# A gMLP and dilated-attention trunk: all operand differences on VectorE, inputs loaded in order of use, and the value norm's root on GpSimd

## The chip, the cores and the metric

The kernel runs on one core of a Trainium2 chip. A core has five engines that work side by side, each in the order of its own queue: TensorE (PE, matmuls), VectorE (DVE), ScalarE (ACT), GpSimd (POOL) and SyncE (SP, which issues DMAs here). They wait for each other through semaphores. The metric is the device time of one execution in microseconds (us). A figure before and a figure after are medians of several executions.

## The reference, cut to what matters

Two layers over 1024 positions with 1024 channels, all in fp32. Layer 0 mixes positions with a gated MLP, layer 1 with dilated attention; each is followed by a dense MLP, and a norm ends it.

```python
for layer in range(DEPTH):                       # DEPTH = 2
    y = _rms_norm(h, mix_norm_g[layer])
    if layer % 2 == 0:
        uv = gelu(y @ w_in); u, v = split(uv)    # the "value" half is v
        v = _layer_norm(v, ln_g, ln_b)
        mixed = einsum('gts,bnsgc->bntgc', tril(w_s), v) + b_s
        y = (u * mixed) @ w_out
    else:
        y = _dilated_attention_mixer(y, ...)     # q, k, v = y @ w_qkv; three dilations; merge; @ w_out
    h = h + y
    y = _rms_norm(h, mlp_norm_g[layer])
    h = h + square(relu(y @ w_up[layer])) @ w_down[layer]
return _rms_norm(h, final_norm_g)
```

`_rms_norm` divides by the root of the mean square plus 1e-6.

## The kernel before, in words

**Numbers.** Each fp32 operand is split into a high part (ACT copies it to the matmul's format) and a low part (DVE subtracts). A product takes three matmuls: high×high, high×low, low×high. A `weight` or `pair().split(...)` therefore costs an ACT and a DVE instruction on a tile of 128x512. `whi`/`wlo` and `wp` are split weights, `y` and `t` split activations, `r` are raw weights as loaded (a pool of four buffers), `h` is the residual, `keep` and `raws` normalized activations, `t…` temporaries of a pool of 11.

**Banks.** Results go to PSUM banks of two pools: `mm` (3) and `at` (5). A bank is free again when ACT or DVE has taken its result out.

**Start.** x arrives transposed, in halves (512 positions) of 8 blocks `h0`…`h7`. The value half v is made in three passes (`gi` 0, 1, 2) over groups of output tiles; the first two also read x. In each of the eight steps k of a pass, `scaled(s, k)` multiplies a block of x with the norm's weights into `y` (and its square into a sum: `Square`, the sums on POOL), two weight halves are loaded and split, and 18 matmuls of 512 columns follow. The norm's 1/rms is not put into y. It is made at the end of the pass (`rms`, four small matmuls, then `rsqrt`) and goes as the scale `rs` into the Gelus (`v_out`), which free the banks for the next pass. `gate_weights` loads and splits the matrices w_s (`wsh`/`wsl`) and makes the bias rows `rb`; `spatial` uses them.

**Seven products.** From the first MLP on, large products are made as seven half-size products in place of eight, with sums and differences of blocks of the operands. `Terms` forms those of the activations: `first` for the first half of the positions (kept in `keep`), `second` for the second half (in `raws`), then four differences for each of four tiles, then `rest`, the splits left over. There are three such stages: before the first MLP, before the attention, before the second MLP. Before the seven products begin, four tiles of each half are made the `classical` way, and their results are evicted (in the MLP `squared`: Relu, Square). Weight sums for the seven products are formed on POOL (`Weights`, L401 to L406). `first_sum` (L750) copies the first product's result out of its bank, for which the next product waits. In the attention, `out` evicts q, k and V tiles (L1079, L1122), a `Unit` is one block of heads: scores from q and k, softmax (L1217, L1219), transposes with `ident`, values.

**Order.** PE's order is written by hand: `Flow` runs generators beside the main loop and places their matmuls by fixed latencies (`LAT`). For the other engines a scheduler picks from what is ready, by priorities; `tc.high_priority(offset=PRIO)` puts an instruction forward. Each engine then works strictly in the order found.

## Time and profile before

| what | value |
| --- | --- |
| median of 3 executions | 2182.33 us (2180.11 to 2182.43) |
| the profiled execution: its time, its span | 2182.13 us, 2180.4 us |
| PE busy | 2121.8 us, 97% of the span |
| DVE, ACT, POOL busy | 1647.1, 1126.3, 600.9 us |
| bytes moved by DMA | 247.04 MB, mean 113 GB/s |
| mean TensorE clock granted | 0.99 |

The profile is one execution. Its span is the stretch from the first to the last instruction. A row of the timeline reads: start, length, engine, line, operation, tile written <- tiles read, shape, number of instructions, and in brackets how long the engine stood idle before and what ended that. `PEclk` in a table by windows is the share of full clock that PE was granted.

### The profile page before, as it was taken

How to read it: one execution, taken by the hardware profiler on the slowest of the kernel's cores; microseconds unless marked ns; L12 is line 12 of the kernel's file. 1: busy time of each engine (PE TensorE's matmuls, PEld its weight loads, DVE VectorE, ACT ScalarE, POOL GpSimd, SP SyncE). 2: the span in 40 equal slices, each digit the busy share in tenths (PEclk: the TensorE clock that was granted, in tenths of full speed). 3: DMA queues.
4: the chain of work that ended last, by engine and by line, in shares of the span. 5: the costliest groups of instructions: out<-in, count | busy, mean ns of one | idle time of the engine just before them, and what ended most of it. 6: DMA issues, size and time to landing. Idle time of an engine off the chain costs nothing.

```text
span 2180.4 us, 30158 instructions
## 1 busy us (share of the span) xinstructions
PE 2121.8 (97%) x10242; PEld 1755.2 (80%) x10242; DVE 1647.1 (76%) x2987; ACT 1126.3 (52%) x2266; POOL 600.9 (28%) x442
## 2 busy tenths in 40 slices
PE   7999999999999999998999999999999999999998
PEld 5888887888878888886888788887878888788887
DVE  5875349676689888878787877878786666988886
ACT  5743225555564444346665656665455555544443
POOL 1100115333223322533212222201343232333345
PEclk9999999999999999999999999999999999999999
DMA  6221213456354444321211111141055543644432
GB/s 222 87 88 45 62 41 96 158 189 198 138 176 160 159 141 137 105 82 39 52 46 46 43 48 45 46 147 62 20 169 193 184 159 113 203 150 146 157 104 78
DMA packets 158814, 247.04 MB, mean 113 GB/s; under 512 B 33481, under 2 KB 47940, under 8 KB 158660
## 3 DMA queue, kind: packets, MB, share of 16 engines
q1 hardware_dynamic: 157760, 243.89, 34.3%
q8 instruction: 80, 1.31, 0.2%
q10 hardware_dynamic: 900, 1.23, 0.2%
q14 instruction: 74, 0.61, 0.1%
HBM read 180.41 MB, written 64.66 MB: 112 GB/s over the span
## 4 chain that ended last, share of the span: by engine, by line
PE 82%; DVE 9%; ACT 3%; issue 2%; DMA 2%; POOL 0%; SPq 0%; DVEq 0%; ACTq 0%; POOLq 0%
PE at L180 41%; PE mm L180 39%; PE at L187 2%; DVE wp L204 2%; DVE t L204 1%; ACT t L1219 1%; ACT wp L203 1%; DVE k L1122 1%; DMA t<-hid 1%; DVE tr L204 0%; DMA r<-in_w_v 0%; DVE h L332 0%; DVE q L1122 0%; DVE h L893 0%; DMA h<-hd 0%
## 5 line engine op out<-in xcount | busy, mean ns | idle before, releaser
L203 ACT ACTIVATE wp<-r 128x512 fp32r<-128x512 f32 (+3 forms) x492 | 295.1, 605 | 458.0 <-PE at L180 287.7
L180 PE MATMUL mm<-y,wp 128*128 128x512 f32 x1608 | 405.2, 398 | 12.8 <-ACT t L750 6.6
L180 PE MATMUL at<-hx,wp 128*128 128x512 f32 x1770 | 413.8, 390 | 3.8 <-DVE wp L204 2.2
L204 DVE TENSOR_TENSOR wp<-r,wp 128x512 fp32r<-128x512 f32 (+3 forms) x492 | 380.9, 778 | 40.1 <-ACT wp L203 36.3
L180 PEld LDWEIGHTS at<-hx,wp 128*128 128x128 f32 x1770 | 331.8, 188 | 75.1 <-DVE h L893 3.3
L180 PEld LDWEIGHTS mm<-y,wp 128*128 128x128 f32 x1608 | 303.2, 191 | 80.4 <-ACT t L750 7.5
L180 PE MATMUL at<-t,wp 128*128 128x512 f32 x1344 | 314.3, 389 | 0.0
L180 PEld LDWEIGHTS at<-t,wp 128*128 128x128 f32 x1344 | 252.7, 188 | 52.7 <-DVE t L756 0.2
L401 POOL TENSOR_TENSOR t<-r 128x512 f32<-128x512 f32 (+3 forms) x78 | 112.8, 1446 | 624.8 <-DMA r<-in_w_dn 270.3
L403 POOL TENSOR_TENSOR r<-r 128x512 f32<-128x512 f32 (+3 forms) x78 | 118.4, 1518 | 326.9 <-DVE wp L204 320.1
L180 PE MATMUL mm<-t,wp 128*128 128x512 f32 x768 | 192.6, 398 | 0.0
L204 DVE TENSOR_TENSOR hx<-t,hx 128x512 fp32r<-128x512 f32 x192 | 179.8, 948 | 5.7 <-ACT hx L203 5.6
L261 POOL TENSOR_TENSOR t<-t 128x512 f32<-128x512 f32 (+1 forms) x54 | 69.1, 1280 | 387.3 <-ACT t L252 385.4
L180 PE MATMUL mm<-hx,wp 128*128 128x512 f32 x708 | 171.8, 389 | 0.0
L180 PEld LDWEIGHTS mm<-t,wp 128*128 128x128 f32 x768 | 141.2, 189 | 29.8
L180 PE MATMUL mm<-y,whi 128*128 128x512 f32 x512 | 158.1, 390 | 0.0
L180 PEld LDWEIGHTS mm<-hx,wp 128*128 128x128 f32 x708 | 132.8, 188 | 28.1 <-DVE b L919 0.6
L893 DVE TENSOR_TENSOR h<-h,at 128x512 f32<-128x512 f32 x144 | 97.5, 679 | 55.4 <-PE at L180 55.3
L180 PE MATMUL at<-y,wp 128*128 128x512 f32 x552 | 138.1, 391 | 0.0
L756 DVE TENSOR_TENSOR t<-t,at 128x512 f32<-128x512 f32 x116 | 79.0, 683 | 74.9 <-PE at L180 74.7
L203 ACT ACTIVATE hx<-t 128x512 fp32r<-128x512 f32 x192 | 118.4, 628 | 27.8 <-DMA t<-hid 23.4
L406 POOL TENSOR_TENSOR r<-r 128x512 f32<-128x512 f32 (+3 forms) x78 | 107.2, 1374 | 79.8 <-issue 54.0
(213 smaller groups left out, 3244.0 us busy)
## 6 DMA issues: line engine op xcount, KB each, us to landing
t<-hid SPq DMA_DIRECT2D x194, 256.0 KB, 5.0
hid<-t SPq DMA_DIRECT2D x140, 256.0 KB, 2.7
r<-in_w_up SPq DMA_DIRECT2D x128, 256.0 KB, 2.8
r<-in_w_dn SPq DMA_DIRECT2D x88, 256.0 KB, 2.7
r<-in_w_qkv SPq DMA_DIRECT2D x72, 256.0 KB, 2.6
hid<-b SPq DMA_DIRECT2D x56, 256.0 KB, 2.7
r<-in_w_v SPq DMA_DIRECT2D x48, 256.0 KB, 3.0
h<-in_xT SPq DMA_DIRECT2D x16, 256.0 KB, 4.5
```

The costliest lines, as they stand in the source:

```text
L180: nc.tensor.matmul(out, lhsT, rhs, **kw)
L187: nc.tensor.transpose(out, src, ident)
L203: nc.scalar.activation(hi, src, AF.Copy)
L204: nc.vector.tensor_tensor(lo, src, hi.bitcast(F32), op=ALU.subtract)
L261: nc.gpsimd.tensor_tensor(self.acc, self.acc, sq, op=ALU.add)
L401: tt(r3, r[0, 0], r[1, 0], op=ALU.subtract)
L403: tt(r[1, 1], r[1, 0], r[0, 0], op=ALU.subtract)
L406: tt(r[0, 0], r[0, 1], r[1, 1], op=ALU.subtract)
L756: nc.vector.tensor_tensor(out, x, y, op=ALU.add)
L893: engine.tensor_tensor(hs[i, s], hs[i, s], src, op=ALU.add)
L1122: nc.vector.scalar_tensor_tensor(lo, a, sc, hi.bitcast(F32), op0=ALU.mult, op1=ALU.subtract)
L1219: nc.scalar.activation(p[:, c], p[:, c], AF.Exp, bias=m, scale=-1.0, accum_out=dn)
```

## The change

1. `rsqrt(..., power=True)` for the first two value norms: in place of Sqrt on ACT and reciprocal on DVE, POOL raises the mean square to the power −0.5 (one instruction on 128x4); the two refinement steps on DVE stay. The norm is made after the first tile of the last step, not after the second.
2. DMAs at the start: block of x, weight half, weight half for each step; the second half of x later; gate weights and their biases by SP after the first pass (before: by ACT's queue within it), and their splits and bias rows within the second pass, put forward. `spatial` waits for `rb_done`.
3. In the second pass the weights of steps 2 to 7 are split behind the sixth Gelu; `scaled` is one step ahead.
4. `Terms.second`: all sixteen differences on DVE, terms 6 and 7 first; `rest` waits for them and splits terms 5 and 4. The copy on POOL goes. Temporaries take the place of spare tiles.
5. MLP: the four Relus first, put forward, then the Squares.
6. The spill of h to memory stands elsewhere in the program; its DMAs have the same neighbours in SP's queue as before.
7. Attention: the second half's tiles are evicted in the order 2, 3, 0, 1.

Where rows differ, the first place is the end of the first pass, on ACT. `whi_556` and, in the new names, `whi_505` are the weights of the second pass's step k=1, `sd` is the root, `vg` the Gelus' output, `rs` the scale. Before:

```order
L203 ACTIVATE whi_556<-r_557 128x512 [waits DMAHW2_49,DVE_49,PE_49]
L203 ACTIVATE whi_556<-r_561 128x512 [waits DMAHW3_49]
L231 ACT_TABLE_LOAD
L231 ACTIVATE sd_417<-at_412,scalars_89 128x4 [waits PE_49]
L588 ACT_TABLE_LOAD
L588 ACTIVATE vg_433<-at_121,rs_104 128x512 [waits DVE_49]
L588 ACTIVATE vg_433<-at_122,rs_104 128x512
```

Now:

```order
L205 ACTIVATE whi_505<-r_510 128x512 [waits DMAHW4_49]
L618 ACT_TABLE_LOAD [waits DVE_49]
L618 ACTIVATE vg_414<-at_123,rs_106 128x512 [waits PE_49]
L618 ACTIVATE vg_414<-at_124,rs_106 128x512 [waits PE_49]
L618 ACTIVATE vg_417<-at_125,rs_106 128x512 [waits PE_49]
L618 ACTIVATE vg_417<-mm_126,rs_106 128x512 [waits PE_49]
```

The root and one table load are gone. The wait for the scale (a DVE semaphore) stood on the first Gelu and stands now on the table load ahead of it.

The start of SP's queue; `h0` to `h2` are blocks of x, `r` weight halves. Before:

```order
L508 DMA h0_92<-in_xT 128x512
L169 DMA r_113<-in_w_v 128x512
L169 DMA r_117<-in_w_v 128x512
L169 DMA r_154<-in_w_v 128x512
L508 DMA h1_93<-in_xT 128x512
L169 DMA r_158<-in_w_v 128x512
L169 DMA r_196<-in_w_v 128x512 [waits DMAHW2_49,DMAHW0_49,DVE_49]
L169 DMA r_200<-in_w_v 128x512 [waits DMAHW3_49,DMAHW1_49,DVE_49]
L169 DMA r_244<-in_w_v 128x512 [waits DMAHW5_49,DVE_49]
```

Now:

```order
L521 DMA h0_94<-in_xT 128x512
L169 DMA r_115<-in_w_v 128x512
L169 DMA r_119<-in_w_v 128x512
L521 DMA h1_95<-in_xT 128x512
L169 DMA r_156<-in_w_v 128x512
L169 DMA r_160<-in_w_v 128x512
L521 DMA h2_96<-in_xT 128x512 [waits DMAHW0_49]
L169 DMA r_191<-in_w_v 128x512 [waits DMAHW2_49,DMAHW1_49,DVE_49]
L169 DMA r_195<-in_w_v 128x512 [waits DMAHW3_49,DVE_49]
```

Each block of x stands now directly ahead of its step's weights; before, five more weight halves, and later the second half of `h0` and `h1`, stood ahead of `h2`.

The first MLP, ACT ahead of `first_sum`, which is the last row of the first piece (L750) and the last but one of the second (L790). L688/L771 are Relus, L689/L773 Squares, L203/L205 splits. Before:

```order
L688 ACTIVATE t_3211<-at_3039 128x512 [waits DMAHW4_49]
L689 ACTIVATE t_3206<-t_3206 128x512 [waits Activation_49]
L688 ACTIVATE t_3216<-mm_3040 128x512 [waits DMAHW5_49]
L689 ACTIVATE t_3211<-t_3211 128x512 [waits Activation_49]
L688 ACTIVATE t_3221<-mm_3041 128x512 [waits DMAHW6_49,PE_49]
L689 ACTIVATE t_3216<-t_3216 128x512 [waits Activation_49]
L689 ACTIVATE t_3221<-t_3221 128x512 [waits Activation_49]
L750 ACTIVATE t_3284<-mm_3267 128x512 [waits DMAHW0_49,PE_49]
```

Now:

```order
L771 ACTIVATE t_3207<-at_3045 128x512 [waits DMAHW7_49]
L771 ACTIVATE t_3209<-mm_3046 128x512 [waits DMAHW0_49]
L771 ACTIVATE t_3211<-mm_3047 128x512 [waits DMAHW2_49,PE_49]
L773 ACTIVATE t_3205<-t_3205 128x512 [waits Activation_49]
L773 ACTIVATE t_3207<-t_3207 128x512 [waits Activation_49]
L773 ACTIVATE t_3209<-t_3209 128x512 [waits Activation_49]
L790 ACTIVATE t_3284<-mm_3267 128x512 [waits PE_49]
L773 ACTIVATE t_3211<-t_3211 128x512 [waits Activation_49]
```

The Relus stand together, and `first_sum` has passed the last Square (and, in rows that follow, one split of the kept tiles).

In the attention PE's order differs at the first scores: unit 0's twelve matmuls on `k0`, `k1`, `q0`, `q1` stood after 21 matmuls of the first two products, and now stand after three of the first (`mm_8808`).

The diff, cut to its core:

```diff
-    def rsqrt(src, scale, out=None):
+    def rsqrt(src, scale, out=None, power=False):
         n = src.shape[1]
-        sd = small.tile([P, n], F32, tag="sd", name="sd")
-        nc.scalar.activation(sd, src, AF.Sqrt, bias=eps, scale=scale)
         v = small.tile([P, n], F32, tag="rv", name="rv")
+        r = small.tile([P, n], F32, tag="rr", name="rr")
+        if not power:
+            sd = small.tile([P, n], F32, tag="sd", name="sd")
+            nc.scalar.activation(sd, src, AF.Sqrt, bias=eps, scale=scale)
         nc.vector.tensor_scalar(v, src, scale, EPS, op0=ALU.mult, op1=ALU.add)
-        r = small.tile([P, n], F32, tag="rr", name="rr")
-        nc.vector.reciprocal(r, sd)
+        if power:
+            nc.gpsimd.tensor_tensor(r, v, mhalf[:, 0:n], op=ALU.pow)
+        else:
+            nc.vector.reciprocal(r, sd)
...
-            for k, two in enumerate(raws):
-                (z0, z1), (y0, y1), t1, t2 = *([t[:, j, :] for j in range(2)] for t in (two, self.kept[k])), spare(), spare()
-                tt(t1, z0, y0, op=ALU.subtract)
-                tt(t2, z1, t1, op=ALU.subtract)
-                nc.gpsimd.tensor_tensor(y0, z1, z0, op=ALU.subtract)
-                nc.gpsimd.tensor_tensor(y1, y1, t2, op=ALU.subtract)
...
+            for k in range(5):
+                if k < 4:
+                    z, y, t = raws[k], self.kept[k], temp()
+                    tt(y[:, 0, :], z[:, 0, :], y[:, 0, :], op=ALU.subtract)
+                    tt(t, z[:, 1, :], y[:, 0, :], op=ALU.subtract)
+                    tt(y[:, 1, :], y[:, 1, :], t, op=ALU.subtract)
+                    sums.append(t)
+                if k:
+                    self.t[6].append(pair("t6").split(sums[k - 1]))
+                yield LAT["tile"]
+            for k in range(5):
+                if k < 4:
+                    tt(raws[k][:, 0, :], raws[k][:, 1, :], raws[k][:, 0, :], op=ALU.subtract)
+                if k:
+                    self.t[7].append(pair("t7").split(raws[k - 1][:, 0, :]))
+                yield LAT["tile"]
+            self.formed = True
...
-                if k == 3:
-                    t4 = temp()
-                    nc.gpsimd.tensor_copy(t4, x[:, 1, :])
...
     def gate_weights():
...
-            nc.scalar.dma_start(w3, w_s[:, 4 * i:4 * i + 4, :])
+            nc.sync.dma_start(w3, w_s[:, 4 * i:4 * i + 4, :])
...
             if gi == 0:
-                load_x(0, k)
-                if k >= 4:
-                    load_x(1, 2 * k - 8)
-                    load_x(1, 2 * k - 7)
-            if gi == 0:
+                x = load_x(0, k)
                 scaled(0, k)
-            w = weight(w_v[k])
-            if gi == 0:
-                if k == 1:
-                    flow.add(gate_weights())
+            if gi == 0 or gi == 1 and k > 1:
+                with tc.issue_after((gelus[5] if gi else x).ins):
+                    w = weight(w_v[k])
+            else:
+                w = weight(w_v[k])
+            if gi == 0 and k > 5:
+                load_x(1, k - 6)
+            if gi == 0 and k == 7:
+                scaled(1, 0)
+                flow.add(gate_weights())
+                flow.pump()
...
-                if k == 7 and e == 2 and f == 1:
+                if k == 7 and e == 2:
                     if i == 0 and gi < 2:
-                        sq[gi].rms(rs[:, 4 * gi:4 * gi + 4])
-                        flow.add(spread_rms(gi), 4000)
-                    else:
+                        if f == 0:
+                            sq[gi].rms(rs[:, 4 * gi:4 * gi + 4], True)
+                            flow.add(spread_rms(gi), 4000)
+                    elif f == 1:
                         v_out(banks, chunks[:i + 1])
...
                 with tc.high_priority(offset=PRIO):
-                    squared(c[q, i, s], b)
+                    nc.scalar.activation(c[q, i, s], b, AF.Relu)
+            for q, i in tiles:
+                nc.scalar.activation(c[q, i, s], c[q, i, s], AF.Square)
...
-        for b, tile in zip(banks, ((0, 0), (0, 1), (0, 2), (1, 0))):
+        outs_ = list(zip(banks, ((0, 0), (0, 1), (0, 2), (1, 0))))
+        for b, tile in outs_[2:] + outs_[:2] if s else outs_:
             out(tile, s, b)
```

More of the change, by code (lines that the diff above doesn't have):

```diff
@@ new lines, in second @@
+            for k in range(5):
[5 more added lines that the diff above has]
+            self.formed = True
+        def rest(self):
+            flow.until(lambda: self.formed)
+            for i, p in ((0, 5), (1, 4)):
+                for x in self.kept:
+                    self.t[p].append(pair(f"t{p}").split(x[:, i, :]))
@@ L996, in trunk, with spill @@
     firsts = []
+    hd = [dram.tile([P, S], F32, tag=f"hd{k}", name=f"hd{k}", bufs=1) for k in range(KT)]
+    def spill():
+        for k in range(KT):
+            nc.sync.dma_start(hd[k], h[k])
     def begin_attention(sq):
```

74 lines of the change are left out of this document (44 added, 30 removed).

## The prediction

> **What bounds the kernel now.** I read the shares of the page first, then TensorE's waits, then the timeline around each long wait.
>
> ```profile
> span 2180.4 us, 30158 instructions
> PE 2121.8 (97%) x10242; PEld 1755.2 (80%) x10242; DVE 1647.1 (76%) x2987; ACT 1126.3 (52%) x2266; POOL 600.9 (28%) x442
> PE at L180 <- ACT y L517: 8.5, 3, 3.7
> PE mm L180 <- ACT t L750: 6.6, 2, 4.3
> PE at L180 <- ACT whi L203: 5.8, 1, 5.8
> PE mm L180 <- ACT t L1079: 5.6, 1, 5.6
> ```
>
> TensorE (PE) is busy 97%, and nothing in the diff takes a large matmul away. So the time can only come from PE's 2180.4 − 2121.8 = 58.6 us of idle, and from what idle time drags behind it, a slower clock. The four wait groups shown (total, times, longest) carry 26.5 us of it. The 5.8 us at the start is the first load and no line of the diff shortens it. The other three groups, in three stages, are where this change works.
>
> ```profile
> core 0: us, PE busy (x) PEld busy (x) DVE busy (x) ACT busy (x) POOL busy (x), PEclk, DMA share, GB/s
> 0.00:20.00 20.00, 10.53 (x37) 8.06 (x37) 10.77 (x18) 11.03 (x18) 2.67 (x8) 0.98 0.77 261
> 29.50:32.90 3.40, 3.19 (x7) 2.20 (x8) 0.95 (x2) 0.47 (x1) 1.46 (x1) 0.50 0.68 208
> 371.00:374.00 3.00, 3.00 (x8) 2.32 (x8) 3.00 (x4) 1.26 (x2) 2.30 (x2) 0.50 1.04 347
> 1592.80:1596.20 3.40, 3.23 (x8) 2.56 (x9) 2.73 (x3) 2.82 (x6) 2.65 (x2) 0.50 0.98 357
> ```
>
> Behind the second stall at the start and behind those of both MLPs the granted clock (PEclk) stands at 0.50 for 3.0 to 3.4 us: half of that, 1.7 us, is lost besides the stall. That is how I price every stall of 2 us or more below.
>
> **The start: input order, gate weights, value norm.**
>
> ```profile
> 19.40 1.58 PE L180 MATMUL at<-whi,y 128*128 128x512 f32 x2 [3.68 <-ACT y L517]
> 29.50 0.79 PE L180 MATMUL at<-whi,y 128*128 128x512 f32 x1 [3.13 <-ACT y L517]
> 57.03 0.50 PE L180 MATMUL at<-whi,y 128*128 128x512 f32 x1 [1.70 <-ACT y L517]
> 58.08 0.50 PE L180 MATMUL at<-whi,y 128*128 128x512 f32 x1 [0.55 <-DVE rv L233]
> ...
> 13.85 1.84 SPq L508 DMA_DIRECT2D h<-in_xT  x2
> ...
> 26.20 0.63 ACT L203 ACTIVATE wsh<-t 128x512 fp32r<-128x512 f32 x1 [4.68 <-POOL t L533]
> 28.73 0.72 ACT L517 ACTIVATE y<-h,vec 128x512 fp32r<-128x512 f32 x1 [0.86 <-DMA h<-in_xT]
> ...
> 11.47 0.62 PE L180 MATMUL at<-whi,y 128*128 128x512 f32 x2
> 40.62 0.62 PE L180 MATMUL at<-whi,y 128*128 128x512 f32 x2
> 44.70 0.62 PE L180 MATMUL at<-whi,y 128*128 128x512 f32 x2
> ```
>
> The first stall: step k=2 of the first pass has its weights, but its block of x is issued at 13.85, behind eight weight loads. The second: ACT works in order, and the split of a gate weight (wsh) holds it for 4.68 us until that weight has landed, with the next y behind it. The change issues x block, weight half, weight half for each step, and puts the gate weights' DMAs and splits behind the pass. A step of PE lasts 44.70 − 40.62 = 4.08 us; its three transfers of 256 KB need 786 KB / 261 GB/s = 3.0 us. So data leads PE, and both stalls go: 3.68 + 3.13 and two half-clock stretches of 1.7. The gate matmuls and their bias rows only move into the second pass. SP has these gate DMAs in its queue now, ahead of the weights of step k=1 of that pass; their four transfers, 1 MB, take 4.0 us at that rate, and four raw buffers let the weights lead by two steps, 8.2 us.
>
> At the end of the first pass comes the norm's root.
>
> ```profile
> 51.22 0.26 ACT L231 ACTIVATE sd<-at,scalars 128x4 f32<-128x4 f32 x1
> 51.50 1.28 ACT L588 ACT_TABLE_LOAD   x1
> 52.79 1.84 ACT L588 ACTIVATE vg<-at,rs 128x512 f32<-128x512 f32 x3
> 51.51 0.16 DVE L233 TENSOR_SCALAR rv<-at 128x4 f32<-128x4 f32 x1 [0.80 <-ACT sd L231]
> ...
> 0.31 0.10 POOL L1607 MEMSET const-float32-0.0<- 128x1 f32 x1 [0.31 <-issue]
> 9.34 1.33 POOL L261 TENSOR_TENSOR t<-t 128x512 f32<-128x512 f32 x1 [7.97 <-ACT t L252]
> ```
>
> Without stalls the pass ends at 11.47 + 7 × 4.08 + about 1 us for the norm's small matmuls = 41. The norm now starts after the first tile of the last step, so its sums are there at about 37.5. Then 0.2 us of VectorE, the power on GpSimd (p), three small VectorE operations (0.6 us), a table load (1.28, which now itself waits for the result; in the old order it had been issued ahead), and the first Gelu's 0.7: done at 40.4 + p. PE needs that bank at 41.6 (one bank is free when the second pass starts). So the norm costs PE max(0, p − 1.2). No row shows a power on GpSimd. The nearest rows bound p: 0.10 us for an instruction on one column, 1.33 us for the same instruction form on 512 columns, where this one has 4. I take p = 1.3, the form's own row, because a power may cost far more for an element than a subtraction; stall 0.1 us. In the second pass the power has the same slack. The rivals below take p beyond these rows. The 1.70 + 0.55 at 57–58 are the Gelu chain's delay of y, which now starts 2.8 us earlier relative to PE (one table load and the root gone, 1.28 + 0.26, and 1.3 from the earlier norm): gone.
> Sum of the start: 3.68 + 3.13 + 0.2 + 1.70 + 0.55 + 3.3 − 0.1 = 12.5 us (0.2 is a small gap behind the second stall). Bounds: 9.3 if a half-clock stretch comes back elsewhere, 13.
>
> The Trainium skill ("TensorE: Matmul & The Clock Gate", § What's actually happening) lets the clock fall only after an idle window of about 3.4 us; by that the stalls of 3.13 and 2.35 would cost no clock and this change 3.4 us less. The rows above show 0.50 behind both, so the measured clock decides.
>
> **The first MLP: differences on VectorE.** Of the 16 differences of a stage (four tiles, four each), 8 move from GpSimd to VectorE, in three stages.
>
> ```profile
> 343.19 3.48 DVE L204 TENSOR_TENSOR t<-b,t 128x512 fp32r<-128x512 f32 x2
> ...
> 1564.21 1.28 DVE L204 TENSOR_TENSOR t<-b,t 128x512 fp32r<-128x512 f32 x2
> ...
> 358.68 1.68 POOL L479 TENSOR_TENSOR keep<-keep,b 128x512 f32<-128x512 f32 x1 [1.23 <-DVE b L477]
> 360.42 0.96 POOL L490 COPY t<-keep 128x512 f32<-128x512 f32 x1
> ...
> 369.31 4.22 PE L180 MATMUL mm<-y,wp 128*128 128x512 f32 x12 [2.35 <-ACT t L750]
> ...
> 367.62 1.16 ACT L689 ACTIVATE t<-t 128x512 f32<-128x512 f32 x2
> ```
>
> VectorE pays 8 × 0.64 = 5.1 us more (two such take 1.28). But while GpSimd subtracts, VectorE's two-input operations slow down: the pair at 343.19 took 3.48 where two take 1.28, so 1.1 us for each of the two GpSimd instructions beside it. Of the stage's eight I count six that meet such an operation: 6.6 us back. So VectorE gains 1.5 us, and the last kept tiles no longer wait for GpSimd's 1.68 + 0.96. On ACT first_sum (L750), for which PE waits from 369.31 − 2.35 = 366.96, now has one Square and one split fewer ahead of it: 1.1 us, taking the Squares' row for both. Together 1.5 + 2.6 + 1.1 = 5.2 us earlier. PE's wait of 2.35 goes, with 2.8 us to spare, and 1.7 of half clock: 4.0 us. Bounds: 1.1 us, if only ACT's order counts, and the whole 4.0. The Relus that now precede all Squares cost nothing: ACT is busy 52%.
>
> **The second MLP** has the same sequence.
>
> ```profile
> 1592.97 4.51 PE L180 MATMUL mm<-y,wp 128*128 128x512 f32 x12 [4.28 <-ACT t L750]
> ```
>
> The same 5.2 us cover its 4.28, with 0.9 us to spare: 4.28 + 1.7 = 6.0 us (bounds 1.1 and 6.0).
>
> **The attention's beginning** is the third stage with differences.
>
> ```profile
> 980.00:1000.00 20.00, 14.35 (x58) 11.53 (x57) 19.54 (x20) 11.30 (x19) 12.66 (x8) 0.89 0.12 39
> 997.35 4.21 PE L180 MATMUL mm<-y,wp 128*128 128x512 f32 x9 [5.65 <-ACT t L1079]
> 1000.11 1.07 DVE L1122 SCALAR_TENSOR_TENSOR k<-at,k 128x512 fp32r<-128x512 f32 x1
> 1009.63 0.33 PE L187 MATMUL at<-ident,t 128*128 128x128 f32 x1 [1.30 <-ACT t L1219]
> ```
>
> VectorE, busy 19.54 of 20 us, bounds this stretch. With about 5.5 us less in front of it (the 5.2 from above, and 0.3 taken for the new order of the evictions), k is split at about 995.7 instead of 1000.11 + 1.07 = 1001.2. But PE's order has changed too: unit 0's scores now follow the first three matmuls of the first product, and wait for k there, where before 18 more matmuls (4.08 us) came first. The 5.65 us stall is therefore not removed but renamed: PE, which in the old order stalls from 997.35 − 5.65 = 991.7, arrives nine matmuls (2.0 us) sooner and waits for k from about 989.7 to 995.7. Net 5.5 − 4.1 = 1.4, and up to 3 us from the small gaps after 1009.63, which have VectorE's lead: I take 2.5, bounds −2 (the small gaps grow) and 6.
>
> **Nothing**: the spill of h keeps its place in SP's queue; load order on SP is otherwise as before; VectorE is 76% busy outside these places.
>
> **Sum**: 12.5 + 4.0 + 6.0 + 2.5 = 25.0 us from the profiled run's 2182.13 (span 2180.4, 1.7 beside it), 2157.1. The median shown is 2182.33, so 2157.
>
> **Rivals.**
> (a) Only the start pays, since VectorE's gain is smaller than its added work: if contention stays (GpSimd's weight sums run in the same stretch, 1.1 us for each), both first_sum stalls keep most of their length; 12.5 + 1.1 + 1.1 + 0 = 14.7: 2168. For it: VectorE was full (19.54 of 20). Against: 10 us of GpSimd work leave the stretch.
> (b) The start pays only in part: the power, or the moved wait of the weight splits behind the sixth Gelu, stalls the second pass. A stall of 4 to 7 us with its half clock eats 6 to 8.5: about 2164. The weight splits of the third step follow the sixth Gelu by two y blocks (0.72 each), a table load (1.28), a root and a copy, some 3.6 us of ACT work, with PE at their heels.
> The Trainium skill ("GPSIMD Engine Reference", § 2.1 Instruction dispatch) has a first call to a freshly loaded GpSimd function pay about 6 us; by that p is over 7 and (b) holds. Here the first TENSOR_TENSOR took 1.33 us, so no such load shows for this form, and none can show for the power.
> (c) Slower: the power takes long for each element. Each us beyond the 1.2 of slack is a us for PE, twice. It decides when the two together exceed 25 + 2 × 1.2 = 27 us, 14 us each; at 18 us each the time is 2191. Four columns against 1.33 us for 512 speak against it.
> (d) Attention's stall goes too, and its small gaps: 3 to 6 us more, 2152.
>
> **How the numbers follow.** Forecast 0.50 (2153 to 2161), (a) 0.20, (b) 0.17, (c) 0.04, (d) 0.06, and 0.03 for no change, that some place not named takes it all back. The range from 2151 to 2171 holds the forecast, (a), (b) and most of (d). A measurement of this kernel tells 0.2% (4.4 us) from nothing: faster 0.92, same 0.04, slower 0.04; since at the edges (a) and (b) can meet, 0.90, 0.06, 0.04.
>
> **What would show it.** Right: no PE idle over 1 us between 6 and 45; clock 1.00 from 20 to 40; the Gelus' first row near 40; no wait for first_sum near 340–360 and 1560–1580 (all later places come earlier by the gain so far); VectorE's differences at 0.68 each; a PE wait of about 5 us for k at the first scores. Wrong: a row of the power over 2 us; a PE wait for whi in the second pass; first_sum still last in both MLPs.

## The result, and the profile after

The changed kernel takes 2167.23 us (median of 4 executions, 2164.51 to 2170.02), the kernel before 2182.38 (4 executions, 2180.11 to 2184.73). The ratio is 0.9928, with a 95% interval of 0.9913 to 0.9944: 0.56 to 0.87% faster. The forecast of 2157 had the sign right and the range of 2151 to 2171 held the time, but its centre is 10 us too low, and the time lies outside the 2153 to 2161 that the forecast's own case covered. The profiled execution after took 2166.1 us.

The page after, its span and its busy times:

```profile
span 2164.4 us, 30121 instructions
PE 2119.0 (98%) x10242; PEld 1755.8 (81%) x10242; DVE 1632.9 (75%) x3010; ACT 1122.5 (52%) x2261; POOL 563.0 (26%) x417
```

PE's idle time fell from 58.6 to 45.4 us, its busy time, with the same 10242 matmuls, by 2.8. Where the 16.0 us of span went is read by stage. I cut both traces at the starts of three groups of rows that both have: the transposes (`ident`) of the norm in the second half of the first MLP, the same ones before the attention, and the first column sums of the norm behind the attention.

| stretch | before | after | gain | forecast |
| --- | --- | --- | --- | --- |
| A: start, value, first half of MLP 1 | 324.0 | 314.4 | 9.6 | 12.5 |
| B: rest of MLP 1 (its `first_sum` lies here) | 632.6 | 628.9 | 3.7 | 4.0 |
| C: attention | 563.5 | 565.7 | −2.2 | 2.5 |
| D: MLP 2 and the final norm | 660.3 | 655.3 | 4.9 | 6.0 |
| sum | 2180.4 | 2164.4 | 16.0 | 25.0 |

So 4.7 of the missing 9.0 us are in the attention, 2.9 at the start, 1.4 in the MLPs. Four of TensorE's longest waits after (total, times, longest):

```profile
PE at L180 <- ACT whi L205: 5.6, 1, 5.6
PE at L180 <- ACT k L1167: 4.9, 1, 4.9
PE at L187 <- ACT t L1265: 4.2, 5, 2.5
PE at L180 <- DVE rb L567: 2.5, 2, 1.3
```

The waits for y (8.5) and for `first_sum` in the MLPs (6.6) are off the list. The wait for `k` is the renamed one that the prediction names; those for L1265 (the first Exps) and for `rb` (the bias rows) are where the time went that it did not count on.

**The start.** A window of the changed kernel; the columns are those of the prediction's table, and the clock is the last but two.

```profile
10.00:40.00 30.00, 30.00 (x138) 24.97 (x137) 21.41 (x28) 17.84 (x31) 10.80 (x9) 1.00 0.82 267
```

PE is busy without a break and at full clock from 10 to 40 us; before, two stalls of 3.68 and 3.13 lay here. The timeline behind it, on PE, ACT, DVE and POOL, in the order of the story. `ones` are the norm's sums, `rv` is the first step of the root, and the `whi`/`wlo` rows ahead of it split the weights of the second pass's step k=1:

```profile
36.42 0.94 PE L180 MATMUL at<-ones,t 128*128 128x1 f32 x8
36.78 1.25 ACT L205 ACTIVATE whi<-r 128x512 fp32r<-128x512 f32 x2 [5.22 <-DMA r<-in_w_v]
37.45 1.31 DVE L206 TENSOR_TENSOR wlo<-r,whi 128x512 fp32r<-128x512 f32 x2 [5.65 <-ACT whi L205]
38.67 0.15 DVE L237 TENSOR_SCALAR rv<-at 128x4 f32<-128x4 f32 x1
38.91 1.02 POOL L239 TENSOR_TENSOR rr<-rv,mhalf 128x4 f32<-128x4 f32 x1 [3.54 <-DVE rv L237]
40.60 1.28 ACT L618 ACT_TABLE_LOAD   x1 [2.57 <-DVE rs L246]
41.89 1.84 ACT L618 ACTIVATE vg<-at,rs 128x512 f32<-128x512 f32 x3
42.72 0.62 PE L187 MATMUL at<-ident,rs 128*128 128x128 f32 x4 [0.43 <-ACT vg L618]
44.37 0.73 PE L180 MATMUL mm<-whi,y 128*128 128x512 f32 x2 [0.19 <-ACT vg L618]
...
53.28 7.67 POOL L267 TENSOR_TENSOR t<-t 128x512 f32<-128x512 f32 x4 [13.35 <-ACT t L258]
56.20 0.64 ACT L258 ACTIVATE t<-h 128x512 f32<-128x512 f32 x1 [2.02 <-POOL t L267]
56.74 0.61 ACT L205 ACTIVATE wsh<-t 128x512 fp32r<-128x512 f32 x1
58.02 3.48 DVE L206 TENSOR_TENSOR wlo<-r,whi 128x512 fp32r<-128x512 f32 x2
62.59 1.12 DVE L567 SCALAR_TENSOR_TENSOR rb<-at,vec,t 128x128 f32<-128x128 f32 x4
63.86 0.30 PE L180 MATMUL at<-wsh,tr 128*128 128x128 f32 x1 [1.32 <-DVE rb L567]
67.28 0.30 PE L180 MATMUL at<-wsh,tr 128*128 128x128 f32 x1 [1.13 <-DVE rb L567]
```

The power takes 1.02 us, so p was bounded well, and the norm's sums are there at 37.36, as forecast (37.5). But VectorE takes them up only at 38.67: the weight splits of the second pass stand ahead in its order, and they had waited for their DMA. ACT stands idle for 2.57 us in front of its table load until the scale is there. The first Gelu is done 0.8 us later than forecast (42.5 for 41.7): waits of 0.43 and 0.19. All behind it on ACT is late too. POOL's four square sums then meet VectorE's work (7.67 us for four; the prediction's row of one at the start had 1.33), ACT idles 2.02 behind them with a split of the second gate matrix (`wsh`, 56.74) next in its order, the two splits of VectorE in front of the bias rows take 3.48 for two, and PE waits twice for `rb`.

**MLP 1.** No wait for `first_sum` is left. ACT and PE there, a later wait, and its window:

```profile
353.93 0.59 ACT L790 ACTIVATE t<-mm 128x512 f32<-128x512 f32 x1
354.49 2.88 PE L180 MATMUL at<-t,wp 128*128 128x512 f32 x12
...
622.88 4.14 PE L180 MATMUL at<-hx,wp 128*128 128x512 f32 x10 [1.60 <-DVE wp L206]
```

```profile
622.00:628.00 6.00, 5.12 (x15) 4.07 (x16) 4.44 (x10) 3.68 (x7) 2.56 (x3) 0.72 0.88 307
```

ACT has the sum out at 354.52, PE has matmuls until 357.37: the 2.8 us to spare that the prediction worked out. Up to 621 us the stage gains 4.4. Then a wait for a weight sum, 1.20 us before and 1.60 now, takes 0.4 back. The clock of 0.72 behind it, where none was lost before, costs little in the end: with the root on ACT (an experiment below) the same wait of 1.59 has no slow clock behind it, and B is only 0.3 us shorter, because PE there waits 0.90 us for `h` a little later (before the change 0.82), a wait that the changed kernel doesn't have.

**The attention's beginning.** The timeline of POOL, ACT, DVE and PE, then a window:

```profile
965.72 3.42 POOL L409 TENSOR_TENSOR r<-r 128x512 f32<-128x512 f32 x1 [29.93 <-issue]
970.54 1.15 ACT L205 ACTIVATE wp<-r 128x512 fp32r<-128x512 f32 x2 [5.84 <-POOL r L412]
971.20 1.30 DVE L206 TENSOR_TENSOR wp<-r,wp 128x512 fp32r<-128x512 f32 x2 [3.20 <-ACT wp L205]
...
981.79 0.58 PE L180 MATMUL at<-k,q 64*128 64x256 f32 x2 [4.88 <-ACT k L1167]
983.24 0.80 PE L180 MATMUL at<-k,q 64*128 64x256 f32 x4 [0.87 <-DVE k L1168]
984.71 5.08 DVE L206 TENSOR_TENSOR t<-keep,t 128x512 fp32r<-128x512 f32 x8
992.20 1.28 ACT L1265 ACT_TABLE_LOAD   x1
994.04 0.33 PE L187 MATMUL at<-ident,t 128*128 128x128 f32 x1 [2.53 <-ACT t L1265]
```

```profile
980.00:1000.00 20.00, 14.16 (x54) 10.25 (x55) 15.79 (x37) 16.05 (x36) 5.42 (x4) 0.71 0.15 44
```

This stage begins 13.3 us earlier than before (943.3 for 956.6). The second part of the scores, which needs k's low half, starts at 983.24; the forecast of 995.7, less 13.3, is 982.4. So the wait for k came as forecast. But with the scores early, PE reaches the first Exp's transposes with 18 matmuls fewer behind it, and the Exp is not 18 matmuls (4.1 us) earlier: eight splits of kept tiles on VectorE and a table load on ACT stand in front of it. PE resumes there at 994.04, which is 2.3 us earlier than before within the stage (1009.63 − 13.3 = 996.4), with 4.1 us less work done: −1.8. A later wait that every kernel here has, 0.7 us for the low half of another `k`, shows where this leads. First the row before the change, then the one after:

```profile
1036.89 0.78 PE L180 MATMUL at<-k,q 64*128 64x128 f32 x10 [0.70 <-DVE k L1122]
1027.44 0.78 PE L180 MATMUL at<-k,q 64*128 64x128 f32 x10 [0.71 <-DVE k L1168]
```

Counted from the start of the stage, that is 80.3 us before and 84.1 after: the beginning loses 3.8 us, and at the end of the stage 2.2 of them are left. Of the 3.8, 3.4 are slow clock. Summed over windows of 1 us (length × (1 − PEclk)), the clock costs 5.1 us up to that wait before and 8.5 after: 3.4 behind the wait for `k`, 3.4 more behind the wait for the first Exp, 1.7 behind small waits. Ahead of all this, with the differences now back to back on VectorE a weight sum of POOL takes 3.42 us (1.28 for the next one, when VectorE is idle), and through ACT's split of POOL's sums VectorE itself stands idle for 3.20.

### The profile page after: what moved, and what is told of

The parts are those of the page before. It is cut to its first block, busy times and chain, and to the rows that moved or that the text cites. A ratio compares the mean times of both kernels' runs of the same rounds, so it can differ in the third digit from the quotient of the medians.

```text
span 2164.4 us, 30121 instructions
## 1 busy us (share of the span) xinstructions
PE 2119.0 (98%) x10242; PEld 1755.8 (81%) x10242; DVE 1632.9 (75%) x3010; ACT 1122.5 (52%) x2261; POOL 563.0 (26%) x417
## 3 DMA queue, kind: packets, MB, share of 16 engines
q8 instruction: 80, 1.31, 0.3%
## 4 chain that ended last, share of the span: by engine, by line
PE 83%; DVE 8%; ACT 4%; issue 3%; DMA 2%; POOL 0%; SPq 0%; DVEq 0%; ACTq 0%; POOLq 0%
PE at L180 42%; PE mm L180 40%; PE at L187 2%; DVE wp L206 1%; ACT t L1265 1%; ACT wp L205 1%; DVE k L1168 1%; DMA r<-in_w_v 0%; DVE h L338 0%; DMA h<-in_xT 0%; DVE h L933 0%; DVE wlo L206 0%; DVE tr L206 0%; DVE q L1168 0%; DVE N L1303 0%
## 5 line engine op out<-in xcount | busy, mean ns | idle before, releaser
L205 ACT ACTIVATE wp<-r 128x512 fp32r<-128x512 f32 (+3 forms) x492 | 295.7, 606 | 463.4 <-PE at L180 290.5
L206 DVE TENSOR_TENSOR wp<-r,wp 128x512 fp32r<-128x512 f32 (+3 forms) x492 | 373.5, 763 | 42.6 <-ACT wp L205 39.0
L796 DVE TENSOR_TENSOR t<-t,at 128x512 f32<-128x512 f32 x116 | 79.2, 684 | 77.7 <-PE at L180 77.4
L205 ACT ACTIVATE hx<-t 128x512 fp32r<-128x512 f32 x192 | 117.8, 628 | 27.3 <-DMA t<-hid 23.4
```

The costliest lines, as they stand in the source:

```text
L205: nc.scalar.activation(hi, src, AF.Copy)
L206: nc.vector.tensor_tensor(lo, src, hi.bitcast(F32), op=ALU.subtract)
L796: nc.vector.tensor_tensor(out, x, y, op=ALU.add)
```

## The experiments

Every run is timed against the kernel before, on the same chip. The kernel before came out 1.9 to 2.9 us slower beside the experiments than beside the first result, while the two medians of the changed kernel agree within 0.5. So the two ratios of that one kernel lie 3.9 us apart, and differences of this size between medians or ratios stay open. Beside the median the table gives the time at full clock: span × mean granted clock, averaged over the executions. The clock is printed with three digits, so one execution's figure is uncertain by 1.1 us. For the kernel before it is 2158.0 to 2158.7 in three groups of executions. Stretches are those of the one profiled execution.

| kernel | median | ratio (95%) | full clock | A | B | C | D |
| --- | --- | --- | --- | --- | --- | --- | --- |
| before | 2182.4 to 2185.3 | 1 | 2158.1 | 324.0 | 632.6 | 563.5 | 660.3 |
| changed | 2167.23 | 0.9928 (0.9913–0.9944) | 2142.2 | 314.4 | 628.9 | 565.7 | 655.3 |
| changed, again (e9) | 2166.76 | 0.9910 (0.9896–0.9925) | 2143.2 | 317.1 | 628.9 | 565.2 | 654.5 |
| root on ACT (e1) | 2161.76 | 0.9900 (0.9887–0.9914) | 2140.6 | 312.7 | 628.6 | 562.8 | 657.0 |
| bias rows early (e2) | 2164.83 | 0.9915 (0.9900–0.9929) | 2144.3 | 314.0 | 628.6 | 566.7 | 653.8 |
| scores late (e3) | 2163.41 | 0.9907 (0.9891–0.9922) | 2141.1 | 318.7 | 628.8 | 559.5 | 657.1 |
| old Relu order (e4) | 2168.22 | 0.9932 (0.9919–0.9944) | 2143.9 | 316.3 | 629.2 | 564.0 | 656.8 |
| old differences (e5) | 2173.97 | 0.9947 (0.9931–0.9963) | 2151.3 | 318.4 | 632.5 | 562.9 | 658.3 |
| before + new differences (e6) | 2175.11 | 0.9949 (0.9931–0.9968) | 2148.9 | 325.3 | 628.2 | 567.1 | 654.2 |
| root on ACT + scores late (e7) | 2160.84 | 0.9884 (0.9867–0.9902) | 2139.2 | 312.1 | 628.6 | 561.4 | 655.7 |
| filler at the scores (e8) | 2164.44 | 0.9902 (0.9885–0.9919) | 2145.5 | 315.7 | 628.9 | 560.4 | 655.6 |
| root on ACT + filler (e10) | 2165.55 | 0.9903 (0.9887–0.9919) | 2143.7 | 311.2 | 628.6 | 562.8 | 656.8 |
| e7 + bias rows early (e11) | 2160.76 | 0.9885 (0.9869–0.9901) | 2139.9 | 315.7 | 628.6 | 562.7 | 655.3 |
| e7 + filler (e12) | 2162.74 | 0.9896 (0.9879–0.9913) | 2141.6 | 311.4 | 628.7 | 560.1 | 657.0 |

Stretches of two profiles of one kernel differ by up to 2.7 us (A, changed and e9), so a difference of that size in the table needs a row behind it. Most of this is clock: the first experiment changes no line of the attention, and its C is 2.9 us shorter than the changed kernel's, with 10.2 us lost to the clock there instead of 13.7.

**The value norm's root, on ACT again.** All else as changed.

```diff
-    sq[gi].rms(rs[:, 4 * gi:4 * gi + 4], True)
+    sq[gi].rms(rs[:, 4 * gi:4 * gi + 4])
```

> The changed kernel, with the value norm's root back on ACT (Sqrt, then reciprocal on DVE); all else stays. Theory: on GpSimd the root takes longer from sums to Gelu, since the power (1.02 us) and then the table load stand one after the other: 4.5 us in the changed kernel's trace (1.3 of it a weight split in front) against 1.7 before, where the Gelu's table loads beside the refinement. With Sqrt the first Gelu comes 1 to 2 us earlier than its 41.89, PE's 0.43 + 0.19 us of waits on it go, and the time falls by about 0.6 us, not measurable: within 2 us of the changed kernel. Rival: taking the root off ACT is a part of the gain, because two table loads (2 x 1.28) and the root hold ACT in front of the Gelus; then the first Gelu comes later than 41.89 and PE waits 2 to 5 us more.

ACT's rows of this kernel:

```profile
35.77 1.24 ACT L205 ACTIVATE whi<-r 128x512 fp32r<-128x512 f32 x2 [5.18 <-DMA r<-in_w_v]
38.32 0.26 ACT L236 ACTIVATE sd<-at,scalars 128x4 f32<-128x4 f32 x1
38.61 1.28 ACT L618 ACT_TABLE_LOAD   x1
39.90 1.85 ACT L618 ACTIVATE vg<-at,rs 128x512 f32<-128x512 f32 x3
51.00 0.62 ACT L205 ACTIVATE wsh<-t 128x512 fp32r<-128x512 f32 x1
```

The Gelu starts at 39.90, not 41.89: with the root on ACT the next table load follows at once and runs while VectorE forms the scale, and with the power it waits for the scale. That is worth 1.0 of the 2.0 us: from the end of the weights' split in front (`whi`) to the Gelu it takes 3.86 to 4.02 us in the seven profiles with the power and 2.87 to 2.95 in the five with the root on ACT. The other 1.0 is that those weights were split 1.0 us earlier in this execution. The Gelu's waits and both `rb` waits vanish. The bias rows come 5.0 us earlier (57.64 for 62.59), more than the Gelu, because ACT's order has changed as well: the split of the second gate matrix (51.00) now stands ahead of the wait for POOL's sums, here 2.65 us, and not behind it. A is 1.7 us shorter, the full-clock time 1.6 (2.6 against e9). The medians say 5 us, the ratios 2.2 against e9; the intervals overlap, so the exact size is open. The power is no gain here: it is short, but it puts GpSimd and two semaphores in the chain and the table load behind them.

**Bias rows earlier.** The second planned pause of 4 us of `gate_weights` goes behind the bias rows.

```diff
-        yield 11000
+        yield 7000
 ...
+        yield 4000
         rb_done.t = flow.t
```

> The changed kernel, with the gate's bias matmuls and rows planned 4 us earlier in the second pass, while the first use of the gates keeps its planned time. Theory: the two waits of 1.32 and 1.13 us on the bias rows (rb) at 63.9 and 67.3 come from these rows standing on DVE behind weight splits that GpSimd's sums slow down (3.48 us for two); started 4 us earlier the rows are done before PE needs them, and about 2.4 us are gained, all before 70 us. Rival: DVE and ACT are full in this stretch, so the wait only passes to the next thing in their queues (a weight split or the gates' operands): PE's idle between 50 and 72 stays at 2 to 3 us.

```profile
58.38 0.50 PE L180 MATMUL at<-wlo,y 128*128 128x512 f32 x1 [1.31 <-DVE wlo L206]
88.61 0.72 PE L180 MATMUL mm<-whi,y 128*128 128x512 f32 x2 [1.73 <-ACT vg L619]
```

The `rb` waits are gone, and a wait for a weight split at 58.38 and one for the next Gelu at 88.61 stand in their place. A is 314.0 for 314.4. The bias rows are only where the second pass's lateness shows; its source lies in front of them. With the root on ACT and the late scores the same edit (below) makes 2160.76 of 2160.84: nothing.

**Scores later.** Only the planner's latency from k to the scores grows, by 4 us.

```diff
-        yield U[0].qk, LAT["qk"]
+        yield U[0].qk, LAT["qk"] + 4000
```

> The changed kernel, with unit 0's scores planned 4 us later, so that PE has 18 matmuls (4.1 us) of the first products before them, as in the kernel before. Theory: the attention's beginning lost 2.2 us because PE's order put the scores too early: PE waits 4.9 + 0.9 us for k, and then 2.5 + 0.6 us for the first Exp with no work left in front. With the scores later the wait for k falls to about 1 us or goes, the Exp's wait stays under 2, and the stretch from 943 to 1509 gets shorter by 4 to 7 us. Rival: VectorE bounds the stretch (splits of the kept terms, q and k); then PE only waits at another place, and the stretch keeps its length within 1 us.

```profile
986.84 2.78 PE L180 MATMUL mm<-y,wp 128*128 128x512 f32 x6 [4.28 <-ACT t L1125]
1001.33 0.33 PE L187 MATMUL at<-ident,t 128*128 128x128 f32 x1 [0.18 <-ACT t L1265]
```

PE now waits for the first product's sum (4.28, before 5.65) as in the old order, and no longer for the Exp (0.18). C is 6.2 us shorter than in the changed kernel, and 4.0 shorter than before the change. The later wait for `k` that was used above comes 78.3 us into the stage, and 78.6 and 79.2 in the other two kernels with late scores and no filler; with early scores and no filler it comes at 83.9 to 84.5 in six profiles, with the old differences at 80.3 and 80.4. The median moved by 3.8 us (3.4 against e9, but 0.7 by the ratios), the full-clock time by 1.1 (2.1); the whole span of this profile does not show C's gain, since its clock is 0.81 between 62 and 80 us, and A with it 318.7. So the loss at the attention's beginning was the place of the scores; how much of the 6.2 is lasting, the medians do not settle.

**The old Relu order.** Relu and Square of a tile together again.

```diff
-                    nc.scalar.activation(c[q, i, s], b, AF.Relu)
-            for q, i in tiles:
-                nc.scalar.activation(c[q, i, s], c[q, i, s], AF.Square)
+                    squared(c[q, i, s], b)
```

> The changed kernel, with Relu and Square of each MLP tile together again, in the old order on ACT; the differences stay on VectorE. Theory A: the two stalls on first_sum went because the differences no longer wait for GpSimd, so ACT's order counts for 1 us: the first MLP keeps its gain (no wait for first_sum), the second has a wait of under 1 us. Theory B: ACT's order did it: the stalls come back with most of their 2.35 and 4.28 us and their half clock, 8 to 10 us slower in all.

2168.22, no wait for `first_sum`, B and D as changed within 1.5 us: no measurable worth once VectorE does all differences.

**The old differences.** `Terms.second` and `rest` as before, all other parts as changed.

```diff
-                    tt(y[:, 0, :], z[:, 0, :], y[:, 0, :], op=ALU.subtract)
-                    tt(t, z[:, 1, :], y[:, 0, :], op=ALU.subtract)
-                    tt(y[:, 1, :], y[:, 1, :], t, op=ALU.subtract)
+                tt(t1, z0, y0, op=ALU.subtract)
+                tt(t2, z1, t1, op=ALU.subtract)
+                nc.gpsimd.tensor_tensor(y0, z1, z0, op=ALU.subtract)
+                nc.gpsimd.tensor_tensor(y1, y1, t2, op=ALU.subtract)
 ...
```

> The changed kernel, with the differences of the three stages half on VectorE and half on GpSimd in their old order. Theory (the differences on VectorE removed both stalls on first_sum): the stalls come back, 2 to 4.5 us each, and the stretches 314 to 621 and 1537 to 1842 get longer by 4 and 5.5 us; the attention's beginning gets back its old length, 2 us shorter. In all 5 to 9 us slower than the changed kernel, about 2174. Rival (the earlier Relus and the order on ACT do it): no stall on first_sum, time within 2 us of the changed kernel.

```profile
362.72 3.03 PE L180 MATMUL mm<-y,wp 128*128 128x512 f32 x12 [1.32 <-ACT t L785]
1583.66 2.84 PE L180 MATMUL mm<-y,wp 128*128 128x512 f32 x6 [2.96 <-ACT t L785]
```

The `first_sum` waits are back at 1.32 and 2.96, where they were 2.35 and 4.28: the rest of the change, ACT's order, is worth 1.0 and 1.3, the prediction's 1.1. B is as before the change (632.5); C is 562.9, below the changed kernel's 565.7.

**Only the new differences, in the kernel before.**

```diff
-                nc.gpsimd.tensor_tensor(y0, z1, z0, op=ALU.subtract)
-                nc.gpsimd.tensor_tensor(y1, y1, t2, op=ALU.subtract)
+                    tt(y[:, 1, :], y[:, 1, :], t, op=ALU.subtract)
 ...
+            flow.until(lambda: self.formed)
```

> The kernel before, with the new differences on VectorE alone; start, norm, gate weights and the order on ACT stay old. Theory: it gains what the changed kernel gained behind 314 us: 4 + 5.5 us in the MLPs, less 2 in the attention: 2175. The start keeps its three stalls. Rival: the parts lean on each other (the sums only come early enough with the new order on ACT): gain under 3 us.

```profile
991.94 0.58 PE L180 MATMUL at<-k,q 64*128 64x256 f32 x2 [4.89 <-ACT k L1126]
1003.40 0.33 PE L187 MATMUL at<-ident,t 128*128 128x128 f32 x1 [2.53 <-ACT t L1224]
```

B and D have the whole gain of the MLPs (628.2, 654.2) and no `first_sum` wait. C has the whole loss (567.1), with the same two waits, 4.89 and 2.53, though the tiles here are evicted in the old order. So the loss belongs to part 4 and not to the eviction order of part 7. Why part 4 moves the scores is read in the code, not measured: `rest` lets `flow` run until the differences are formed, which carries the planner's clock ahead of its list of due matmuls. At full clock the two halves add up: removing the new differences costs 9.1 us (8.1 against e9), they alone bring 9.2, and all other parts alone 6.8 (2158.1 − 2151.3).

**Root on ACT and late scores together.** The edits of the first and third experiments.

> The changed kernel with the root on ACT and unit 0's scores 4 us later together. Theory: the two places lie 900 us apart and have nothing in common, so the gains add: 5.5 + 3.8 us by the medians (1.7 + 6.2 by the single profiles' stretches): 2157 to 2160. Rival: a part of either gain was a lucky placing of the half-clock stretches, and the two together gain under 6 us: 2161 or more.

2160.84 us, a ratio to before of 0.9884 (0.9867 to 0.9902), the best with e11. It beats the changed kernel by 6.4 us in the medians (5.9 against e9) and by 3 to 4 at full clock; the interval lies below that of the changed kernel's first runs and overlaps that of e9. The two gains by the medians, 5.5 and 3.8, did not add up to 9.3: the expected 2157 to 2160 was missed by a little, and a part of either may have been the place of slow-clock stretches, as the rival had it. The only long wait in the middle is the old one in the attention, 4.3.

**Filler at the scores.** Twenty extra matmuls whose result is overwritten keep PE busy in front of unit 0's scores, while it waits for k.

```diff
+        if u is U[0] and j == 0:
+            w = xa.t[1][0].hi
+            for _ in range(20):
+                nc.tensor.matmul(sb[1], w[:, 0:P], w, start=True, stop=True)
```

> The changed kernel with 20 idle matmuls (512 columns, 4.4 us, into the scores' own bank before they are written) ahead of unit 0's first scores, where PE waits 4.9 us for k; the results are not changed. Theory (a stall's price is the half clock behind it, and keeping PE busy saves it): the granted clock between 980 and 1000 stays near 1, and 3 us or more are gained in the stretch from 943 to 1509. Rival A (VectorE sets the pace there, a faster PE only waits longer for the first Exp): the clock stays up, the stretch keeps its length within 1 us. Rival B: the fillers run late and add their own time, up to 4 us slower.

```profile
977.50 4.70 PE L1250 MATMUL at<-y 128*128 128x512 f32 x20
```

```profile
980.00:990.00 10.00, 8.56 (x39) 6.41 (x38) 9.29 (x14) 9.54 (x16) 2.59 (x2) 0.83 0.19 53
```

The wait for k shrinks to 0.45 + 0.99 and C to 560.4. The clock holds in part: 0.83 in this window, and 5.1 us are lost to it up to the later wait for `k`, where the changed kernel loses 8.5. That wait comes at 80.9 and not at 84.1, although PE now does 4.4 us of filler as well, so the theory has some truth: the filler fills a wait and saves slow clock behind it. By the ratio to before the whole gains 1.7 us on e9, which its interval does not tell from nothing.

**The changed kernel again**, unchanged, to see how a second set of executions and a second profile of it come out.

> The changed kernel itself once more, beside the others of this call: 2164 to 2170, ratio to the kernel before 0.991 to 0.994. If instead its ratio is under 0.990, the differences of the earlier calls to it (root on ACT 5.5 us, late scores 3.8 us) are in part drift between calls.

2166.76 for 2167.23. The ratio of 0.9910 is just inside what was expected. Its profile has the same waits at the start (1.31 and 0.61 for `rb`), but the clock between 62 and 80 us is 0.81; in the first one, behind 1.32 and 1.13, it is 1.00. First the row of the first profile, then that of this one:

```profile
62.00:80.00 18.00, 15.55 (x85) 12.89 (x84) 16.25 (x37) 8.97 (x16) 1.84 (x1) 1.00 0.47 142
```

```profile
62.00:80.00 18.00, 16.08 (x69) 13.05 (x69) 16.11 (x38) 8.06 (x14) 1.85 (x1) 0.81 0.41 136
```

18 × 0.19 = 3.4 us of clock: with 0.5 less for the second wait, that is about A's difference of 2.7 between the two profiles.

**Root on ACT with the filler** (edits of the first and the filler experiment).

> Root on ACT, and the 20 idle matmuls ahead of unit 0's first scores in place of later scores. Theory: as the stretch from 943 to 1509 was 5 us shorter with the idle matmuls as well, this is worth as much as the later scores: 2158 to 2162. Rival: the idle matmuls only helped through the order they gave on ACT (table load ahead of the first softmax) or by chance of the clock: 2161 to 2163, the stretch no shorter than 562.

2165.55, against 2161.76 without the filler (ratios 0.9903 and 0.9900), and C is 562.8 in both: no gain.

**Root on ACT, late scores and early bias rows.**

> Root on ACT, later scores, and the bias rows 4 us earlier. Theory: with the root on ACT there is no wait on the bias rows left to take away, so this is worth nothing more: within 1.5 us of root and scores alone (2160.8), and the stretch up to 313 does not get shorter. Rival: the bias rows are still close to the path, and 1 to 2 us more are gained.

2160.76 for 2160.84: no gain.

**Root on ACT, late scores, and 18 filler matmuls in front of the first product's sum**, where the 4.3 us wait is.

```diff
+            f, z = at_bank(), x.t[1][0].hi
+            for _ in range(18):
+                nc.tensor.matmul(f, z[:, 0:P], z, start=True, stop=True)
```

> Root on ACT, later scores, and 18 idle matmuls (4 us) in the wait of 4.3 us that is left behind the first product of the attention, where PE waits for ACT to free a bank. Theory: the wait stays, but the clock behind it stays up: 1.7 to 3.4 us gained, 2157 to 2159. Rival: the clock falls none the less (short waits and small matmuls follow), and nothing is gained or 1 us lost.

```profile
979.54 1.68 PE L180 MATMUL mm<-y,wp 128*128 128x512 f32 x6 [0.33 <-ACT t L1125]
991.89 0.33 PE L187 MATMUL at<-ident,t 128*128 128x128 f32 x1 [2.95 <-ACT t L1268]
```

The wait of 4.28 becomes 0.33, and a wait for the Exp of 2.95 returns twelve us later; 2162.74 for 2160.84. The later wait for `k` comes at 81.6, 3.0 us later than without the filler (78.6). Here VectorE and ACT set the pace: once the scores are late, filling PE's wait gains nothing more.

## Why the prediction was right, and where it was off

**Input order: right.** Both stalls for y are gone and the clock is 1.00 from 10 to 40 us. The 1.70 + 0.55 at 57 are gone too. No run has the new input order alone; that it did this is read from the trace.

**"The gate matmuls and their bias rows only move": the step that failed at the start.** They moved into the second pass with VectorE and ACT at PE's heels, and PE waits 1.32 + 1.13 for them. Those 2.45 and the Gelu's 0.62 are the 2.9 missing in A within 0.2; the row of the power, forecast at 1.3, is 1.02. The rival that a moved wait in the second pass eats a part of the start's gain was near: 3 us of it, not 6 to 8.5. The norm's sums came on time (37.36 for "37.5"), but the "0.2 us of VectorE" behind them began 1.3 us late, behind weight splits of the second pass, which the sum left out. And the table load, which the prediction saw now waiting for the result, had its cost counted at 1.28 but not the lateness that all of ACT inherits. The first experiment shows that half: with the root on ACT all these waits go.

The Trainium skill ("GPSIMD Engine Reference", § 2.1 Instruction dispatch) puts about 6 us on the first call of a freshly loaded GpSimd function; the trace does not show it, the two powers take the same:

```profile
L239 POOL TENSOR_TENSOR rr<-rv,mhalf x2: 1022/1022/1022, 38.9 to 83.6; 128x4 f32<-128x4 f32 x2
```

**The MLPs: right.** Forecast 4.0 and 6.0, measured 4.4 up to 621 us and 5.5 up to the final norm, 3.7 and 4.9 to the end of the stretches. ACT's order was worth 1.0 and 1.3 (forecast 1.1) with the old differences, and nothing measurable with the new ones. The rival that only ACT's order pays is out: with the new differences alone the waits are gone, with the old ones they stay.

**The attention: the renamed wait was right, the term was mis-sized,** +2.5 for −2.2, just beyond its lower bound of −2. The prediction priced k (forecast 982.4, PE resumed at 983.24) and then took "up to 3 us from the small gaps after 1009.63, which have VectorE's lead". They do not have it: the first Exp, behind the kept splits and a table load, came 2.3 us earlier where PE came 4.1 us earlier, so the gap of 1.30 grew to 2.53 + 0.64. The slow clock behind that larger gap was in no term: the stage loses 13.7 us to the clock, before 10.2, and without it C would be 1.3 shorter. With the scores late, C gains 4.0 on before.

**The half clock: priced too surely, and the step that cost most.** 6.7 of the 25.0 us were half-clock stretches taken as gone with their stalls. The time lost to the clock by stage, summed over windows of 1 us in the profiles:

| stretch | before | after | after, again (e9) | gain forecast |
| --- | --- | --- | --- | --- |
| A | 3.4 | 0.0 | 3.4 | 3.3 |
| B | 1.7 | 1.7 | 0.0 | 1.7 |
| C | 10.2 | 13.7 | 13.7 | 0 |
| D | 7.1 | 6.1 | 3.8 | 1.7 |
| sum | 22.4 | 21.5 | 20.9 | 6.7 |

The stretches behind the named stalls did go, but others came: at the first Exp, behind the wait at 622 us, and in e9 behind the first `rb` wait. Between the two profiles compared above 0.9 of the 6.7 arrived, so of the missing 9.0 us 5.8 are clock; the other 3.2 are work and waits (18.3 forecast, 15.1 measured), 3.0 of them at the start. Over all executions, span less full-clock time was 23.5 to 26.2 us before and is 21.6 to 23.3 after: between 0.2 and 4.6 us arrived. The prediction priced a lower clock only for stalls of 2 us or more, and only for stalls that go; here waits of 1.3 to 1.6 us had one behind them (0.72 at 622 us; 0.50 in e9 at 66 us).

So all large stalls of the start and of the MLPs went as worked out, and the small waits, the attention and the clock took 10 us back. That the range still held the time is partly luck: 2167 lies above the forecast's own case and above the rival in which the start pays only in part (2164), next to the 2168 of the rival in which only the start pays. That rival did not happen, since both waits for `first_sum` went.

## What to carry to other kernels

When a stall goes because an engine ahead got faster, ask of the very next thing that the waiting engine meets whether it has moved earlier by as much; if PE arrives with less work done, the difference comes back as a new gap. A short instruction moved to an idle engine can still be late if it puts two semaphores and another engine's table load behind it: leave it where the next step of the chain can start without waiting. A stall that goes takes its slow clock with it only if no new wait comes up: count the new waits too, also those of little more than 1 us. Where two engines besides PE set the pace, filling PE's gaps gains little or nothing; shorten those engines' work, or move PE's wait to where least hangs on it, as the late scores did.

## What the runs showed of the hardware

- Much of the spread between executions of one kernel is clock. The changed kernel's four times go from 2164.5 to 2170.0 with clocks from 0.990 to 0.988, and its full-clock times from 2141 to 2143, 2142 and 2143 in the mean of two sets. It is not all: eleven executions of the kernel before go from 2181 to 2192, and at full clock still from 2155 to 2161, with 1.1 us of rounding.
- The slow clock comes in pieces. In all fourteen profiles, at every place where PEclk is below 1 except for the last 11 us of a profile, the loss (1 − PEclk, summed over windows of 1 us) is 1.7, 3.4 or 5.1 us: a stretch of 3.4 us at 0.50, once, twice or three times.
- A lower clock in front of a wait for another engine can cost almost nothing: 1.7 us of it in the changed kernel at 622 us lengthened B by 0.3 against e1 (628.9 for 628.6), since a wait of 0.90 behind it went.
- The clock fell to 0.50 (66 to 72 us in the second profile of the changed kernel) behind a wait of only 1.31 us at 64.2; the next wait, 0.61, lies within the slow stretch. In the first profile it stayed at 1.00 behind 1.32 and 1.13. The Trainium skill ("TensorE: Matmul & The Clock Gate", § What's actually happening) says that the window that watches for activity runs freely, so that the moment of a change varies between executions; that agrees with these two rows. Its idle window of about 3.4 us does not: the wait is shorter. What decides after short waits stays open.
- GpSimd and VectorE slow each other in both directions. The prediction's rows have VectorE at 1.74 for each beside POOL, 0.64 alone; with the differences back to back on VectorE, a weight sum on POOL took 3.42 us, where the next one of the same size took 1.28 with VectorE idle. The changed kernel's own differences on VectorE took 0.67 to 0.69 each in the mean in the first two stages, as forecast (0.68); in the third, four of the sixteen took 0.95.
